# Layer norms of a two-layer decoder trunk: staged dummy products, squares on two engines, x from two queues, and no GpSimd work beside the norms

## The chip, the core and the metric

The kernel runs on one core of one Trainium2 chip. A core has five engines with a queue of instructions each: PE (matrix products; PEld is its weight load), DVE (vector), ACT (scalar and activation functions), POOL (GpSimd), and SP, which here only issues DMAs. The metric is the time of one execution in microseconds (us); before the change it is 2330.64 us, the median of 3 runs (2330.39 to 2331.34).

## The reference

Two layers (DEPTH = 2) over x of 256 tokens by 2048 channels, in float32. Each layer does

```
h = RMSNorm(x, pre_norm)                 # over the 2048 channels of a token
proj = h @ w_in                          # 2048 x 17120: three mixers and the merge gates
y_a = SSD(proj), y_b = RWKV-7(proj), y_c = sparse attention(proj)
merged = sum_i sigmoid(g_i + b_i) * (y_i @ w_branch_i)
x = x + RMSNorm(merged @ w_out, post_norm)
```

The change touches only the places where a token's sum of squares is taken and used: the norm ahead of the first layer, and the pair of norms between the two layers.

## The kernel before, in words

The 256 tokens are two halves of 128 (c = 0 and 1); a half of x is a tile of 128 partitions by 2048, named ya (c = 0) and yb (c = 1), which is worked on in four quarters of 512 columns (q = 0 to 3). A norm is: the squares of each quarter summed into a column of n_s (`square`, L808), a chain of eight one-column DVE instructions that makes 1/sqrt (`rstd`, L812, tiles n_x), the scaling of each quarter by it, and the transposition by PE (products with the identity in cst, 128 x 128, into PSUM tiles psa). From psa ACT makes hh (the rounded value) and DVE makes hl (the remainder), 16 pieces each of 128 x 256 (`prenorm`, L833).

All large products are done in three parts of a rounded format: hh with the rounded weight whi, hl with whi, and hh with the remainder wlo, accumulated in PSUM tiles psg. The weights come as 512 KB pieces (wraw) through SP's queue, in the order of use; each is two halves, of which `prepare` (L692) makes whi and wlo, each with four buffers. In the code before, the first three halves of the program have whi made by DVE and the others by ACT; wlo is made by POOL for the first six halves of a layer (PL = 6) and by DVE for the others.

PE's clock is one of two levels, 1.2 and 2.4 GHz; the profile's column PEclk gives it as 0.50 and 1.00. `warm` (L1615) issues products whose result is not used: six of 512 columns at the start, eight of 256 columns between the layers.

What order the instructions stand in is decided by a planner (`Program.issue`, L329): every call is recorded with its rank and the tiles that it reads and writes, and each engine then takes, at its own modelled time, the ready instruction of lowest rank (ranks: -2 and -1 before 0 before 1, 2, 3; equal ranks by the order in the code). `prenorm` has rank -1. The order is fixed when the program is built, and each engine works through its own list in that order. At the end of a layer `output` (L1552) makes the last columns of the product with w_out for the first half of the tokens, then for the second, and `add` (L1597) adds the normed result to x, half by half, writes it out and sums the next norm's squares.

Of the kernel before, what the change touches and what calls it, by code (L numbers as in the profile page):

```python
# [10 lines left out]
F32 = mybir.dt.float32  # L11
# [4 lines left out]
AF = mybir.ActivationFunctionType  # L16
OP = mybir.AluOpType
AX = mybir.AxisListType

DM, S, NL = 2048, 256, 2  # L20
# [9 lines left out]
LA = 2  # L30
# [2 lines left out]
PG = 3  # L33
KT = 2
KW = 2
PL = 6
KK = 14


# [65 lines left out]
CST = {"ident": 0, "tri": 128, "cbias": 256, "inv": 384, "sign": 385}  # L105
NCST = 386
# [98 lines left out]
class Program:  # L205
# [123 lines left out]
    def issue(self, tc):  # L329
# [21 lines left out]
        for i in range(N):  # L351
            if not left[i]:
                add(i)
# [18 lines left out]
        while len(order) < N:  # L372
# [74 lines left out]
            for j in users[i]:  # L447
                left[j] -= 1
                to = ops[j][0]
                ready[j] = max(ready[j], t + busy if to == e == "PE" else end[i] + (LT if to == "PE" else 0.0))  # L450
                if j in batch and batch.get(i) is not batch[j]:
                    batch[j][1] -= 1
                    batch[j][2] = max(batch[j][2], ready[j])
                if not left[j]:
                    add(j)
# [25 lines left out]
class Trunk:  # L481
# [82 lines left out]
        return y  # L564


    def setup(self):
        nc, v = self.nc, self.v
        self.ones = self.T([128, 128], "ones")
        v.memset(self.ones, 1.0)  # L570
        self.cst = self.T([128, NCST], "cst")
        self.io.dma_start(self.cst, self.cst_d[:, 0:NCST])
        c = lambda n, w=128: self.cst[:, CST[n]:CST[n] + w]
        self.ident, self.tri, self.cbias = c("ident"), c("tri"), c("cbias")
        self.blkr, self.onesr = [self.T([128, 128], n, dt=F32R) for n in ("blkr", "onesr")]
        blk = self.t1(128)
        self.io.dma_start(blk, self.cst_d[:, NCST:NCST + 128])
        v.tensor_copy(self.blkr, blk)
        v.tensor_copy(self.onesr, self.ones)

        self.zl = self.T([128, 10, S], "zl", dt=F32R)
        self.g.memset(self.zl.bitcast(F32), 0.0)

        self.zp = self.T([128, 6, 512], "zp")
        self.g.memset(self.zp, 0.0)

        self.sbd = self.T([128, 2, 128], "sbd")
        v.memset(self.sbd, 0.0)

        self.vd = self.T([128, 8, 128], "vd")  # L590
        self.g.memset(self.vd, 0.0)
        self.ut = self.T([128, 8, 64], "ut")
        v.memset(self.ut, 0.0)
# [98 lines left out]
    def prepare(self):  # L692

        self.prog.rank, was = 1, self.prog.rank
        while len(self.ready) <= LA and (self.raw or self.nraw < NL * self.wst.shape[1]):
            self.prog.rank = 1
            while len(self.raw) < 3 and self.nraw < NL * self.wst.shape[1]:
                self.fetch()
            r = self.raw.pop(0)
            of = 2 * self.wst.shape[1]  # L700
            n, self.nhalf = self.nhalf, self.nhalf + 1
            self.prog.rank = 1 if n > LA else -1
            if n % of < of - KK:
                hi = self.T([128, 512], "whi", WB, F32R)
                lo = self.T([128, 512], "wlo", WB, F32R)
                if n > LA:
                    self.s.activation(hi, r, AF.Copy)
                else:
                    self.v.tensor_copy(hi, r)
                (self.v if n % of >= PL else self.g).tensor_tensor(lo, r, hi.bitcast(F32), op=OP.subtract)  # L710
                self.ready.append((hi, lo))
                continue

            n = n % of - (of - KK)
            cut = lambda a: [a[:, 0:256], a[:, 256:512]]
            if n < KT:
                hi, lo = cut(self.t2(512, dt=F32R)), cut(self.t2(512, dt=F32R))
            elif n >= KK - KW:
                hi, lo = cut(self.T([128, 512], "whi", WB, F32R)), cut(self.T([128, 512], "wlo", WB, F32R))
            else:  # L720
                hi, lo = [[self.t1(dt=F32R) for _ in range(2)] for _ in range(2)]
            for e, q, h, w in zip((self.v, self.g), cut(r), hi, lo):
                self.s.activation(h, q, AF.Copy)
                e.tensor_tensor(w, q, h.bitcast(F32), op=OP.subtract)
            self.ready.append(list(zip(hi, lo)))
        self.prog.rank = was
# [70 lines left out]
            self.v.scalar_tensor_tensor(lo, src, scale, hi.bitcast(F32), op0=OP.mult, op1=OP.subtract)  # L797


    def residual(self, src):  # L800

        x = [self.T([128, DM], n) for n in ("ya", "yb")]
        for c in range(2):
            for q in range(4):
                self.io.dma_start(x[c][:, 512 * q:512 * q + 512], src[128 * c:128 * c + 128, 512 * q:512 * q + 512])
        return x

    def square(self, ss, x):  # L808

        self.s.activation(self.t2(512)[:, :x.shape[1]], x, AF.Square, scale=DM ** -0.5, accum_out=ss)  # L810

    def rstd(self, ss):  # L812
        v = self.v
# [783 lines left out]
    def add(self, x, u, ss, last, c):  # L1597
        v, s = self.v, self.s
        r = self.rstd(ss[c])
        so = self.sums(4)  # L1600
        cuts = [512 * i for i in range(5)]
        if last and c:
            cuts.insert(4, 1792)
        for q, qs in enumerate(slice(i, j) for i, j in zip(cuts, cuts[1:])):
            if c and q == 1:
                s.activation(u[c][:, qs], u[c][:, qs], AF.Copy, scale=r)
                self.g.tensor_tensor(x[c][:, qs], x[c][:, qs], u[c][:, qs], op=OP.add)
            else:
                v.scalar_tensor_tensor(x[c][:, qs], u[c][:, qs], r, x[c][:, qs], op0=OP.mult, op1=OP.add)
            self.io.dma_start(self.out[128 * c:128 * c + 128, qs], x[c][:, qs])  # L1610
            if not last:
                self.square(so[:, q:q + 1], x[c][:, qs])
        return so
# [6 lines left out]

    def run(self):
        self.prog.rank = 0
        x = u = self.residual(self.x_d)
        ss = [self.sums(4) for _ in range(2)]
        for c in range(2):
            for q in range(4):
                self.square(ss[c][:, q:q + 1], x[c][:, 512 * q:512 * q + 512])
        self.setup()
        self.warm(6, self.ones[:, None, :].to_broadcast([128, 4, 128]))
        self.prepare()  # L1630
        for l in range(NL):
            self.layer_setup(l)
            if l:
                self.prog.rank = 3
                self.warm(8, x[0][:, 1536:1792])
                self.prog.rank = 2
            h = self.prenorm(x, ss, u)
            if l == 0:
                self.rope_tables()
            m = self.layer(l, h)  # L1640
            x, ss, u = self.output(l, m)
        self.prog.issue(self.tc)
# [16 lines left out]
```

## Time and profile before

| what | value |
|---|---|
| median of the timed runs | 2330.64 us |
| the profiled execution, its own time | 2333.83 us |
| span of the profiled execution | 2332.1 us |
| PE busy in the span | 2295.8 us (98%), 18750 products |
| DVE, ACT, POOL busy | 1712.8, 1405.9 and 797.6 us (73%, 60%, 34%) |
| mean PE clock granted | 0.993 |

The profile is of one execution. A row of a timeline gives start, duration, engine, line, operation and tiles (out<-in), and in brackets how long the engine stood idle before it and what ended that. All rows have line 460, the planner's own, so rows are told apart by tiles.

### The profile page before, as it was taken

Reading aid. Unit: us, or ns where it says so; the run is one execution under the profiler, and the core shown is the slowest. Engines: PE = TensorE matmul, PEld = TensorE weight load, DVE = VectorE, ACT = ScalarE, POOL = GpSimd, SP = SyncE. Lnnn points to the kernel's source line nnn. Section 1 sums busy time; section 2 is a strip of 40 time slices with the busy share of each in tenths; the row PEclk is TensorE's granted clock in tenths of the full one; section 3 lists DMA queues with packets and bytes.
Section 4 is the critical chain, followed back from the end, with each engine's and each line's share of the span. In section 5 each row is a group of like instructions: output and inputs, shape, how many; then the busy total and the mean of one; then the engine's idle time right before and its main releaser. Section 6 shows DMA issues by size and latency. Waiting matters only on the chain. (4 is left out here: it accounts for less than half of the span.)

```text
span 2332.1 us, 50202 instructions
## 1 busy us (share of the span) xinstructions
PE 2295.8 (98%) x18750; PEld 2239.0 (96%) x18750; DVE 1712.8 (73%) x3468; ACT 1405.9 (60%) x2994; POOL 797.6 (34%) x1241
## 2 busy tenths in 40 slices
PE   8999999999999999999989999999999999999998
PEld 7999999999999999998889999999999999999987
DVE  7988998878995555556577789888789755555565
ACT  5876666775654454545467675776756544544453
POOL 3468564755210010101235776538341100110011
PEclk8999999999999999999999999999999999999999
DMA  5545453454445665556544545444454556655563
GB/s 187 177 159 184 126 175 118 138 159 152 142 163 187 221 207 185 200 185 214 170 145 157 177 152 161 125 138 156 141 162 140 172 188 219 206 189 191 183 216 127
DMA packets 149588, 396.14 MB, mean 170 GB/s; under 512 B 47904, under 2 KB 51936, under 8 KB 149088
## 3 DMA queue, kind: packets, MB, share of 16 engines
q1 hardware_dynamic: 149344, 392.94, 51.8%
q8 instruction: 147, 2.41, 0.4%
q14 instruction: 97, 0.79, 0.1%
HBM read 386.55 MB, written 6.32 MB: 168 GB/s over the span
## 5 line engine op out<-in xcount | busy, mean ns | idle before, releaser
L460 DVE TENSOR_TENSOR wlo<-wraw,whi 128x512 fp32r<-128x512 f32 x1352 | 1018.6, 756 | 528.3 <-ACT whi L460 515.6
L460 ACT ACTIVATE whi<-wraw 128x512 fp32r<-128x512 f32 x1361 | 857.4, 631 | 754.1 <-PE psg L460 707.9
L460 PE MATMUL psg<-hh,whi 128*128 128x256 f32 (+1 forms) x4224 | 1190.5, 282 | 1.0 <-ACT hh L460 1.0
L460 PE MATMUL psg<-hh,wlo 128*128 128x256 f32 (+1 forms) x4224 | 1190.1, 282 | 0.0
L460 PE MATMUL psg<-hl,whi 128*128 128x256 f32 (+1 forms) x4224 | 1186.6, 281 | 0.0
L460 PEld LDWEIGHTS psg<-hh,whi 128*128 128x128 f32 x4224 | 798.0, 189 | 2.4 <-ACT hh L460 1.6
L460 PEld LDWEIGHTS psg<-hl,whi 128*128 128x128 f32 x4224 | 798.3, 189 | 1.5 <-issue 0.8
L460 PEld LDWEIGHTS psg<-hh,wlo 128*128 128x128 f32 x4224 | 797.0, 189 | 1.8 <-issue 0.4
L460 POOL TENSOR_TENSOR t<-t,t 128x256 fp32r<-128x256 f32 (+22 forms) x506 | 340.5, 676 | 283.0 <-ACT t L460 170.4
L460 POOL TENSOR_TENSOR b_nm<-b_nm,t 128x256 f32<-128x256 f32 x64 | 51.2, 800 | 722.9 <-DVE t L460 714.9
L460 PE MATMUL psg<-t,whi 128*128 128x256 f32 x1536 | 280.6, 283 | 0.0
L460 PEld LDWEIGHTS psg<-t,whi 128*128 128x128 f32 x1536 | 238.9, 191 | 0.0
L460 PE MATMUL psg<-t,wlo 128*128 128x256 f32 x768 | 217.3, 283 | 0.0
L460 ACT ACTIVATE t<-t 64x256 fp32r<-64x256 f32 (+5 forms) x436 | 178.9, 416 | 35.1 <-DVE t L460 20.5
L460 PEld LDWEIGHTS psg<-t,wlo 128*128 128x128 f32 x768 | 147.1, 192 | 0.0
L460 POOL TENSOR_TENSOR t<-t,d 128x60 f32<-128x60 f32 (+24 forms) x248 | 108.1, 436 | 65.0 <-DMA d<-diag 27.6
L460 ACT ACTIVATE t<-psa 128x256 f32<-128x256 f32 (+5 forms) x230 | 93.8, 424 | 43.1 <-PE psa L460 41.8
L460 PE MATMUL psg<-whi,hh 128*128 128x512 f32 (+1 forms) x268 | 98.1, 366 | 0.0
L460 PE MATMUL psg<-wlo,hh 128*128 128x512 f32 (+1 forms) x268 | 97.7, 365 | 0.0
L460 PE MATMUL psg<-whi,hl 128*128 128x512 f32 (+1 forms) x268 | 97.1, 365 | 0.0
L460 PE MATMUL psa<-t,t 128*128 128x256 f32 (+1 forms) x384 | 87.5, 288 | 2.8 <-ACT t L460 2.2
L460 PE MATMUL psa<-t,zp 128*128 128x128 f32 (+1 forms) x448 | 82.3, 298 | 0.0
(248 smaller groups left out, 2503.4 us busy)
## 6 DMA issues: line engine op xcount, KB each, us to landing
wraw<-in_wst SPq DMA_DIRECT2D x688, 512.0 KB, 3.4
d<-diag SPq DMA_DIRECT2D x32, 128.0 KB, 3.8
t<-diag SPq DMA_DIRECT2D x16, 256.0 KB, 3.9
d<-in_wst SPq DMA_DIRECT2D x8, 512.0 KB, 4.9
ya<-in_x SPq DMA_DIRECT2D x8, 256.0 KB, 5.1
yb<-in_x SPq DMA_DIRECT2D x8, 256.0 KB, 6.1
b_nm<-in_post SPq DMA_DIRECT2D x2, 1024.0 KB, 4.8
out_x<-ya SPq DMA_DIRECT2D x8, 256.0 KB, 2.8
```

What stands on the lines that cost most here:

```text
L460: ops[i][2](*ops[i][3], **ops[i][4])
```

## The change

At the start, x is requested by two queues: quarters 1 and 3 of the second half of the tokens by ACT's queue, all others by SP's, and the constants (cst) are requested between the two halves of x. The squares of quarters 1 and 3 of each half go to DVE (as a product with a summed output), those of 0 and 2 stay on ACT. After the six dummy products come three further groups (2, 3 and 3, of 256 columns), each fed by the output of one of DVE's squares, so that it can't start before that. Between the layers the eight dummies are followed by groups of 5, 4 and 4, fed by quarters 0, 2 and 3 of the second half's new x.

All wlo are made by DVE and all whi by ACT (PL is gone), except in a layer's last pieces, and the first three halves have rank 0 where they had -1. In `add`, quarter 1 of the second half goes through ACT and POOL in the last layer alone; between the layers DVE does it. One constant (blkr) has rank 2.

```diff
@@ setup
+        self.prog.rank = 2
         blk = self.t1(128)
         self.io.dma_start(blk, self.cst_d[:, NCST:NCST + 128])
         v.tensor_copy(self.blkr, blk)
         v.tensor_copy(self.onesr, self.ones)
+        self.prog.rank = 0
@@ prepare
-            self.prog.rank = 1 if n > LA else -1
+            self.prog.rank = 1 if n > LA else 0
...
-                if n > LA:
-                    self.s.activation(hi, r, AF.Copy)
-                else:
-                    self.v.tensor_copy(hi, r)
-                (self.v if n % of >= PL else self.g).tensor_tensor(lo, r, hi.bitcast(F32), op=OP.subtract)
+                self.s.activation(hi, r, AF.Copy)
+                self.v.tensor_tensor(lo, r, hi.bitcast(F32), op=OP.subtract)
@@ residual
+            if c and between:
+                between()
             for q in range(4):
-                self.io.dma_start(x[c][:, 512 * q:512 * q + 512], src[128 * c:128 * c + 128, 512 * q:512 * q + 512])
+                (queues or [self.io])[c * q % 2 if queues else 0].dma_start(x[c][:, 512 * q:512 * q + 512], src[128 * c:128 * c + 128, 512 * q:512 * q + 512])
@@ add
-            if c and q == 1:
+            if c and last and q == 1:
@@ run
-        x = u = self.residual(self.x_d)
+        x = u = self.residual(self.x_d, [self.io, self.s], self.tables)
...
+                z = x[c][:, 512 * q:512 * q + 512]
+                if q % 2:
+                    sq.append(self.t2(512))
+                    self.v.tensor_tensor_reduce(out=sq[-1], in0=z, in1=z, scale=1.0 / DM, scalar=0.0, op0=OP.mult,
+                                                op1=OP.add, accum_out=ss[c][:, q:q + 1])
+                else:
+                    sq.append(self.square(ss[c][:, q:q + 1], z))
         self.setup()
         self.warm(6, self.ones[:, None, :].to_broadcast([128, 4, 128]))
+        for t, n in ((sq[3], 3), (sq[5], 2), (sq[7], 3)):
+            self.warm(n, t[:, 0:256])
...
-                self.warm(8, x[0][:, 1536:1792])
+                for n, a in ((8, x[0][:, 1536:1792]), (5, x[1][:, 0:256]), (4, x[1][:, 1024:1280]), (4, x[1][:, 1792:2048])):
+                    self.warm(n, a)
```

Since the planner decides on all of it at once, the order shifts elsewhere too: in the first layer many instructions stand in other places, in the second layer the lists come back to nearly the same order.

On DVE at the start of the program, before the change, the scaling of yb and the rounding of weights (whi) stand among each other, and the first remainders hl follow at once; wlo isn't in this list, it is POOL's.

```order
28 L460 TENSOR_SCALAR ya_63<-ya_63,n_x_111 128x512
29 L460 CAST whi_88<-wraw_86 128x512
30 L460 CAST whi_90<-wraw_86 128x512
31 L460 TENSOR_SCALAR yb_64<-yb_64,n_x_115 128x512
32 L460 CAST whi_93<-wraw_87 128x512
33 L460 TENSOR_SCALAR yb_64<-yb_64,n_x_115 128x512
34 L460 SCALAR_TENSOR_TENSOR hl_107<-psa_116,par_95,hh_106 128x256
35 L460 SCALAR_TENSOR_TENSOR hl_107<-psa_117,par_95,hh_106 128x256
36 L460 TENSOR_SCALAR d_oka_100<-par_95 128x8
```

In the changed list the same engine has its first wlo (wlo_92) only behind the last of the 16 hl; the first hl is row 41 there.

```order
56 L459 SCALAR_TENSOR_TENSOR hl_110<-psa_125,par_98,hh_109 128x256
57 L459 SCALAR_TENSOR_TENSOR hl_110<-psa_126,par_98,hh_109 128x256
58 L459 CAST t_66_128<-t_65_127 128x256
59 L459 SCALAR_TENSOR_TENSOR hl_110<-psa_125,par_98,hh_109 128x256
60 L459 SCALAR_TENSOR_TENSOR hl_110<-psa_126,par_98,hh_109 128x256
61 L459 TENSOR_TENSOR wlo_92<-wraw_89,whi_91 128x512
62 L459 TENSOR_TENSOR wlo_94<-wraw_89,whi_93 128x512
63 L459 TENSOR_TENSOR wlo_97<-wraw_90,whi_96 128x512
```

On PE at the same place, before, products of the first block (psg_134) stand among the transposes (psa), and the first with wlo is row 24.

```order
19 L460 MATMUL psg_134<-hh_106,whi_88 128x256
20 L460 MATMUL psa_120<-cst_76,yb_64 128x128
21 L460 MATMUL psa_120<-cst_76,ya_63 128x128
22 L460 MATMUL psa_120<-cst_76,yb_64 128x128
23 L460 MATMUL psg_134<-hl_107,whi_88 128x256
24 L460 MATMUL psg_134<-hh_106,wlo_89 128x256
25 L460 MATMUL psg_134<-hh_106,whi_88 128x256
26 L460 MATMUL psa_121<-cst_76,ya_63 128x128
```

In the changed list two products of the first block (rows 25 and 26) come ahead of the last twelve transposes, and the third needs wlo_92, with all others behind it.

```order
35 L459 MATMUL psa_126<-cst_65,ya_63 128x128
36 L459 MATMUL psa_126<-cst_65,yb_64 128x128
37 L459 MATMUL psa_126<-cst_65,ya_63 128x128
38 L459 MATMUL psa_126<-cst_65,yb_64 128x128
39 L459 MATMUL psg_137<-hh_109,wlo_92 128x256
40 L459 MATMUL psg_137<-hh_109,whi_91 128x256
41 L459 MATMUL psg_137<-hl_110,whi_91 128x256
42 L459 MATMUL psg_137<-hh_109,wlo_92 128x256
```

Between the layers, PE's changed list has eleven of the thirteen new dummies (into psa_3142, psa_3143 and psa_3144) ahead of the first transpose of the second half (row 8797); b_nm there is the scaled second half, yc the first.

```order
8789 L459 MATMUL psa_3141<-ya_2907,ones_76 128x256 x8
8790 L459 MATMUL psa_3142<-yb_2908,ones_76 128x256 x5
8791 L459 MATMUL psa_3143<-yb_2908,ones_76 128x256
8792 L459 MATMUL psa_3157<-cst_65,yc_2910 128x128
8793 L459 MATMUL psa_3143<-yb_2908,ones_76 128x256 x3
8794 L459 MATMUL psa_3144<-yb_2908,ones_76 128x256
8795 L459 MATMUL psa_3158<-cst_65,yc_2910 128x128
8796 L459 MATMUL psa_3144<-yb_2908,ones_76 128x256
8797 L459 MATMUL psa_3155<-cst_65,b_nm_2911 128x128
```

Before, nothing but two transposes of yc stood between the eight dummies of ya and that first transpose; the thirteen dummies of the second half are new.

## Rows read from the trace of the kernel before

**Rows 1.** Stretches, start: length; PE, PEld, DVE, ACT, POOL busy (instructions); clock, DMA, GB/s.

```profile
9.00:13.00 4.00, 0.75 (x6) 0.53 (x5) 3.41 (x20) 2.46 (x8) 0.00 (x0) 1.00 1.04 394
13.00:22.10 9.10, 6.53 (x24) 4.95 (x25) 7.91 (x14) 7.55 (x19) 8.04 (x10) 0.50 0.69 240
22.10:26.60 4.50, 4.50 (x23) 4.50 (x22) 3.59 (x13) 2.90 (x8) 1.19 (x3) 0.50 0.01 2
```

**Rows 2.** PE's psg products by stretch: busy (count), clock, DMA share, GB/s.

```profile
0.00:22.00 22.00, 2.13 (x5) 0.79 0.78 263
22.00:26.60 4.60, 3.59 (x14) 0.50 0.01 3
26.60:30.00 3.40, 3.40 (x31) 1.00 0.02 5
30.00:40.00 10.00, 10.00 (x88) 1.00 0.59 209
```

**Rows 3.** Timeline of DVE at the start.

```profile
9.57 1.28 DVE L460 TENSOR_SCALAR ya<-ya,n_x 128x512 f32<-128x512 f32 x3
...
11.34 0.16 DVE L460 TENSOR_REDUCE n_x<-n_s 128x1 f32<-128x5 f32 x1 [0.49 <-ACT t L460]
...
13.77 1.50 DVE L460 TENSOR_SCALAR yb<-yb,n_x 128x512 f32<-128x512 f32 x1
...
20.44 1.66 DVE L460 SCALAR_TENSOR_TENSOR hl<-psa,par,hh 128x256 fp32r<-128x256 f32 x4 [1.19 <-ACT hh L460]
```

**Rows 4.** Timeline of ACT at the start.

```profile
10.52 0.63 ACT L460 ACTIVATE t<-yb 128x512 f32<-128x512 f32 x1
...
12.89 1.34 ACT L460 ACTIVATE yb<-yb,n_x 128x512 f32<-128x512 f32 x2 [1.06 <-DVE n_x L460]
```

**Rows 5.** Timeline of POOL at the start.

```profile
13.60 5.62 POOL L460 TENSOR_TENSOR wlo<-wraw,whi 128x512 fp32r<-128x512 f32 x4 [6.73 <-DVE whi L460]
```

**Rows 6.** DMA issues of the first 12 us: size, us to landing.

```profile
cst<-in_cst SPq DMA_DIRECT2D x1, 193.0 KB, 6.4
```

**Rows 7.** A stretch between the layers, columns as in the first group.

```profile
1173.60:1176.90 3.30, 3.28 (x16) 3.28 (x17) 1.88 (x5) 2.88 (x7) 0.00 (x0) 0.50 0.01 2
```

**Rows 8.** Timeline of DVE between the layers.

```profile
1155.89 2.74 DVE L460 SCALAR_TENSOR_TENSOR ya<-yc,n_x,ya 128x512 f32<-128x512 f32 x4
...
1164.18 0.16 DVE L460 TENSOR_REDUCE n_x<-n_s 128x1 f32<-128x6 f32 x1 [1.18 <-ACT t L460]
...
1167.06 1.41 DVE L460 SCALAR_TENSOR_TENSOR yb<-b_nm,n_x,yb 128x512 f32<-128x512 f32 x2
1168.39 0.42 DVE L460 TENSOR_TENSOR b_nm<-psa,b_nm 128x256 f32<-128x256 f32 x1
...
1171.60 0.16 DVE L460 TENSOR_REDUCE n_x<-n_s 128x1 f32<-128x5 f32 x1 [1.46 <-ACT t L460]
```

**Rows 9.** Timeline of POOL between the layers.

```profile
1163.87 2.50 POOL L460 TENSOR_TENSOR wlo<-wraw,whi 128x512 fp32r<-128x512 f32 x2 [15.02 <-ACT whi L460]
```

**Rows 10.** Timeline of ACT between the layers.

```profile
1173.13 1.34 ACT L460 ACTIVATE b_nm<-yb,n_x 128x512 f32<-128x512 f32 x2 [1.57 <-DVE n_x L460]
```

**Rows 11.** Timeline of PE: dummies and first transpose between the layers, two waits later.

```profile
1163.26 3.62 PE L460 MATMUL psa<-ya,ones 128*128 128x256 f32 x16
...
1173.62 0.48 PE L460 MATMUL psa<-cst,b_nm 128*128 128x128 f32 x1 [4.43 <-DVE b_nm L460]
...
1227.76 0.41 PE L460 MATMUL psa<-adt,cst 128*128 128x32 f32 x2 [1.74 <-DVE adt L460]
...
1719.95 0.48 PE L460 MATMUL psa<-cst,t 128*128 128x128 f32 x1 [3.62 <-DVE t L460]
```

**Rows 12.** Stretches, same columns: the first layer's body, and behind a wait.

```profile
28.00:1163.00 1135.00, 1129.78 (x9302) 1105.24 (x9301) 848.88 (x1720) 692.95 (x1469) 390.92 (x612) 1.00 0.53 172
1227.70:1231.50 3.80, 3.74 (x19) 3.70 (x20) 2.38 (x7) 1.12 (x3) 0.00 (x0) 0.55 0.68 253
```

**Rows 13.** DVE's own wlo by line: shortest/median/longest ns, first and last start, forms.

```profile
L460 DVE TENSOR_TENSOR wlo<-wraw,whi x1352: 626/692/1782, 29.5 to 2298.2; 128x512 fp32r<-128x512 f32 x194
```

More of the change, by code (lines that the diff above doesn't have):

```diff
@@ L35 @@
 KW = 2
-PL = 6
 KK = 14
@@ L564, in rsqrt, with tables @@
         return y
+    def tables(self):
+        self.cst = self.T([128, NCST], "cst")
+        self.io.dma_start(self.cst, self.cst_d[:, 0:NCST])
+        c = lambda n, w=128: self.cst[:, CST[n]:CST[n] + w]
+        self.ident, self.tri, self.cbias = c("ident"), c("tri"), c("cbias")
     def setup(self):
@@ L570, in setup @@
         v.memset(self.ones, 1.0)
[L571 to L574, printed above, removed]
         self.blkr, self.onesr = [self.T([128, 128], n, dt=F32R) for n in ("blkr", "onesr")]
+        self.prog.rank = 2
         blk = self.t1(128)
@@ L797, in split, with residual @@
             self.v.scalar_tensor_tensor(lo, src, scale, hi.bitcast(F32), op0=OP.mult, op1=OP.subtract)
-    def residual(self, src):
+    def residual(self, src, queues=None, between=None):
         x = [self.T([128, DM], n) for n in ("ya", "yb")]
         for c in range(2):
+            if c and between:
+                between()
             for q in range(4):
-                self.io.dma_start(x[c][:, 512 * q:512 * q + 512], src[128 * c:128 * c + 128, 512 * q:512 * q + 512])
+                (queues or [self.io])[c * q % 2 if queues else 0].dma_start(x[c][:, 512 * q:512 * q + 512], src[128 * c:128 * c + 128, 512 * q:512 * q + 512])
         return x
     def square(self, ss, x):
-        self.s.activation(self.t2(512)[:, :x.shape[1]], x, AF.Square, scale=DM ** -0.5, accum_out=ss)
+        t = self.t2(512)[:, :x.shape[1]]
+        self.s.activation(t, x, AF.Square, scale=DM ** -0.5, accum_out=ss)
+        return t
     def rstd(self, ss):
@@ L1622, in run @@
         self.prog.rank = 0
-        x = u = self.residual(self.x_d)
+        x = u = self.residual(self.x_d, [self.io, self.s], self.tables)
         ss = [self.sums(4) for _ in range(2)]
+        sq = []
         for c in range(2):
             for q in range(4):
-                self.square(ss[c][:, q:q + 1], x[c][:, 512 * q:512 * q + 512])
+                z = x[c][:, 512 * q:512 * q + 512]
[5 more added lines that the diff above has]
+                    sq.append(self.square(ss[c][:, q:q + 1], z))
         self.setup()
         self.warm(6, self.ones[:, None, :].to_broadcast([128, 4, 128]))
+        for t, n in ((sq[3], 3), (sq[5], 2), (sq[7], 3)):
+            self.warm(n, t[:, 0:256])
         self.prepare()
```

## The prediction

> **What bounds the kernel now.** The table of busy times comes first: PE is busy for 2295.8 of 2332.1 us, and nothing in the change alters a product whose result is used. So it can move only where PE waits or works at half clock. I read the stretches next: in the first layer's body (28 to 1163 us) PE's idle time is 1135.00 - 1129.78 = 5.2 us [rows 12], so there is little to win there, and something to lose. What is left is the start and the seam between the layers. At the start PE is almost idle from 9 to 13 us (0.75 us busy), then 13 to 26.6 us pass at clock 0.50, the last 4.5 of them with PE full [rows 1]. At the seam PE waits 4.43 us for the scaled b_nm [rows 11] and then works 3.3 us full at 0.50 [rows 7]. The timelines of DVE, ACT and POOL then say what the norms wait for.
>
> All sums are made on the profiled execution, 2333.83 us (span 2332.1 and 1.7 outside it); it lies 3.2 us over the median 2330.64, and I carry the differences over to the median.
>
> **The start.** The progress of the first products (psg) is the measure. Before, 5 + 14 + 31 are begun by 30.0 us; up to three stand in two stretches, so about 47. From there the rate is 88 in 10 us, 0.117 us each [rows 2].
>
> What the norm waits for before: ACT's last square starts at 10.52 [rows 4] and the sum of the second half at 11.34 [rows 3]; the scaling starts at 12.89 on ACT [rows 4], so the chain takes 1.5 us.
>
> The x transfers: cst (193.0 KB) [rows 6] now goes ahead of the second half. At 394 GB/s [rows 1] that is 0.198 MB / 394 = 0.5 us later for the last quarter, and I keep it whole although two queues issue, because the share of the DMA engines already is 1.04 in that stretch [rows 1]. The sum then comes at about 11.9, the scale at 13.45.
>
> Beside this row stands a rule of the Trainium skill ("DMA: Bandwidth & Descriptors", section "Issuing engines are not separate DMA queues"): transfers issued by several engines go through the same 16 DMA engines and interleave, so several issuers save issue time only. The 1.04 agrees with it, and by the rule the last quarter doesn't land sooner. Were it otherwise and the two queues added their rates, x would land some 0.8 us sooner and the forecast would be 2328.7.
>
> DVE's four squares: no row shows this operation. The nearest are DVE's wlo at 0.69 (same size) [rows 13] and DVE's scaling beside POOL's work at 1.50 [rows 3]. Four cost 2.8 to 6.0 us; I take 0.75 each, by the row without company, since POOL now has nothing there. At that price three are done while x is still landing, and the last lies beside ACT's square of 0.63 [rows 4]: cost 0. At 1.50 the last ends 0.8 later than ACT's and the one ahead of it may push it: up to 1.3 us. Below nothing it can't cost beyond the 0.6 of one ACT square.
>
> Behind the sum: on DVE the three ya scalings at 0.427 (1.28 for three) [rows 3], two of yb at the same price (0.86; it was 1.50 for one beside POOL [rows 3, 5]), two small ones (0.2): 13.45 + 2.3 = first hl at 15.75. Sixteen hl at 1.66 / 4 = 0.415 [rows 3] are 6.6, four small instructions 0.5: 22.9. Only now comes wlo_92 (it was POOL's, at 1.4 us each, 5.62 for four [rows 5]; DVE's takes 0.69 [rows 13]): 23.6. In PE's new order the third product waits for it, so PE's list is free at about 23.75. Then all weights and remainders are there. At full clock the 47th product begins 44 x 0.117 = 5.15 later, at 28.9: 1.1 us sooner than before.
>
> But the clock: PE now has dummies to about 12.6 (eight of the kind that took 3.62 us between the layers [rows 11], 9.0 + 3.6), and from there to 23.75 only some 34 short instructions, about 4 us of work in 11. Before, with PE busy 6.53 of 9.10 us between 13.0 and 22.1, the clock was 0.50 all along, and it was regained only behind 4.5 us of full work [rows 1]. So I expect half clock by 23.75, and to be regained by full work as long as in the three places seen: 4.5 [rows 1], 3.3 [rows 7], 3.8 us at 0.55 [rows 12]. In each, half the time is lost: 1.65 to 2.25, I take 2.0. The start costs **-1.1 + 2.0 = +0.9**. Its ends: -1.1 with the clock up, -1.8 with earlier x too; +2.5 with slow squares.
>
> **The seam.** POOL's two wlo run from 1163.87 for 2.50 us [rows 9]. Beside them the first half's norm needs 1164.18 to 1167.02, where yb's scaling follows at 1167.06 [rows 8]: 2.84 instead of the 1.5 of the start. Without POOL: one wlo more on DVE (1163.9 to 1164.6), the chain to 1166.05, three adds at 2.74 / 4 = 0.685 [rows 8] to 1168.1, the product's evacuation at 0.42 [rows 8] to 1168.5, the fourth add (before on ACT and POOL) to 1169.15, ACT's square and the sum at about 1170.05: 1.55 sooner than 1171.60 [rows 8]. By the same 2.02 from sum to first b_nm transpose (1171.60 to 1173.62 [rows 8, 11]) this is ready at 1172.05.
>
> PE's eight dummies end at 1163.26 + 3.62 = 1166.9 [rows 11]; eleven new ones at 0.45, held up by the adds that feed them, go to about 1171.9. So they hardly delay the transpose, PE isn't idle for long, and the half clock at 1173.6 to 1176.9 [rows 7] goes: 1.65. Next in line is ACT, whose two b_nm scalings take 1.34 [rows 10]; behind them it makes hh from about 1173.0. The fifth product of the next block, at 1178.7 before (my reading of PE's products there), comes at 1176.7: **-2.0**. Its ends: -2.8 if the whole of 1.55 and 1.65 is kept, -0.5 if the dummies overrun or the clock falls all the same.
>
> **Elsewhere.** Six wlo per layer go from POOL to DVE, 4.2 us each layer of an engine that is busy 848.88 of 1135 [rows 12]: hidden as long as nobody waits for it. The wait for adt (1.74) and for t (3.62) in the second layer [rows 11] have the same neighbours in the lists afterwards: they stay. Layer 0's new order I price at 0, with its loss as a rival.
>
> **Sum.** +0.9 - 2.0 + 0 = -1.1: 2332.7 on the profiled execution, **2329.5 us** on the median.
>
> **Rivals.**
> *A, slower: layer 0's new order brings a wait.* DVE has the wlo and also the small chains (dt, adt) for which PE waits at [rows 11]; layer 0, with 5.2 us idle [rows 12], has no such wait now, and its list is the one that is reshuffled. One like adt's costs 1.74 and half of the 3.8 us at half clock behind it [rows 12], 3.5; one like t's 3.62 + 1.7 = 5.3. Time 2333.0 to 2334.8, with two 2336.5. It decides from about 1 us of net loss in layer 0. Against it: PE's order is planned against the same costs as before, and 75% of DVE's time is used, not all.
> *B, the dummies at the start hold the clock*: -1.1 instead of +0.9, 2327.5, with x sooner or both ends of the seam 2326. For it: the clock was 1.00 in 9 to 13 with PE nearly idle [rows 1], so it doesn't fall at once. Against it: 13 to 22.1 at 0.50 with PE 72% busy.
> *C, the seam gives little*: the thirteen dummies, fed one after the other by the adds, push the transposes, or the clock falls in the hh stage behind them. -0.5 instead of -2.0: 2331.0.
> That layer 0's new order wins is bounded by the 5.2 us idle in it; I give it no case, but room in the range.
>
> **How the numbers follow.** Forecast 0.47, A 0.18, B 0.20, C 0.15. What a measurement here can tell from no change is about 0.2%, 4.7 us: below 2326.0 and above 2335.3. Faster: half of B and some of the forecast's lower tail (layer 0 a little better), 0.18. Slower: most of A, 0.14. Within: 0.68. The forecast's own range is 2327.3 to 2332; with B below and A above, and the unknown price of the squares, 2325.3 to 2335.5.
>
> **What would show it.** Start: the sum of the second half at 11.9 (sooner: the queues do add up), DVE's squares near 0.75, first hl at 15.8, wlo_92 at 22.9, PE's third product at 23.75, clock 0.50 before and for some 4 us behind it, then 1.00. If the clock is 1.00 there, B. Seam: no POOL, the sum at 1170, the first b_nm transpose at 1172 behind the dummies, no stretch at 0.50. Elsewhere: the waits of 1.74 and 3.62 still there, and layer 0's idle time near 5 us. The forecast is wrong if layer 0 shows a wait of over 1.5 us, if DVE's squares take twice as long, or if the first block's third product stands at another time than 23 to 24.5 us.

## The result, and the profile after

The changed kernel takes 2350.6 us (median of 4 runs, 2347.32 to 2351.51) beside 2330.99 us of the kernel before (4 runs): ratio 1.008, 95% interval 1.0064 to 1.0096. It is slower by 19.6 us; the forecast was 2329.5, the range ended at 2335.5.

To see where the time went I cut each profiled execution at three instructions that every kernel has: the 48th psg product at the start, the first dummy of the seam, and the 48th psg product behind it. The body is the first layer between the first two. Idle is its length less PE's busy time; half is the time at clock 0.50 in it, by the trace's clock record.

| us | 48th product at | body | idle in it | half in it | seam | from there to the end |
|---|---|---|---|---|---|---|
| before | 30.03 | 1133.23 | 5.22 | 0 | 20.49 | 1148.33 |
| after | 30.18 | 1151.16 | 15.55 | 17.1 | 18.26 | 1145.95 |
| difference | +0.2 | **+17.9** | +10.3 | +17.1 | -2.2 | -2.4 |

The differences add up to 13.5, which is that of the two spans (2345.6 and 2332.1). The medians lie 19.6 apart: the profiled run of the changed kernel is its shortest, at 2347.32, and that of the kernel before is longer than its median, so some 6 us of the difference stand in neither trace. In the body PE's busy time is 7.6 us longer for the same work; 14.2 us of work at half clock (4.3, 3.4 and 6.4 us in the three stretches at 0.50) accounts for about 7 of them. The two places that the change edits come out as forecast, at the start even to a few tenths. First DVE there, with start, duration and what it did:

```profile
8.59 0.69 DVE L459 CUSTOM_DVE_ANT_0 t<-ya 128x512 f32<-128x512 f32 x1
...
12.15 0.15 DVE L459 TENSOR_REDUCE n_x<-n_s 128x1 f32<-128x5 f32 x1
...
15.77 1.66 DVE L459 SCALAR_TENSOR_TENSOR hl<-psa,par,hh 128x256 fp32r<-128x256 f32 x4
...
22.80 3.02 DVE L459 TENSOR_TENSOR wlo<-wraw,whi 128x512 fp32r<-128x512 f32 x4
```

The square costs 0.69 (I took 0.75), the sum of the second half comes at 12.15 (11.9), the first hl at 15.77 (15.75), wlo_92 at 22.80 (22.9). Where [rows 3] had the sum at 11.34, it is 0.8 later. PE has its dummies to 12.35, then little, and waits for that wlo:

```profile
8.73 3.62 PE L459 MATMUL psa<-t,ones 128*128 128x256 f32 x16
...
23.53 0.58 PE L459 MATMUL psg<-hh,wlo 128*128 128x256 f32 x1 [3.81 <-DVE wlo L459]
```

The clock is at 0.50 from 22.97 to 26.39, so PE works at it for 2.86 us behind the wait. At the seam there is no POOL and no half clock (stretches; columns as in [rows 1]), and what [rows 11] showed as a wait of 4.43 us for b_nm is now dummies up to the first transpose:

```profile
1184.80:1190.00 5.20, 5.20 (x26) 4.23 (x25) 4.77 (x15) 3.29 (x9) 0.00 (x0) 1.00 0.81 251
1190.00:1195.20 5.20, 5.20 (x43) 4.88 (x43) 4.35 (x11) 5.04 (x14) 0.00 (x0) 1.00 0.15 53
```

```profile
1187.58 1.89 PE L459 MATMUL psa<-yb,ones 128*128 128x256 f32 x8
...
1189.97 0.33 PE L459 MATMUL psa<-cst,b_nm 128*128 128x128 f32 x1
```

The loss is in the body, where the change edits nothing but who makes six wlo. What PE waits for there, between 30 and 1160 us (total, times, longest), before:

```profile
PE psa L460 <- ACT zp L460: 1.1, 2, 0.6
PE psa L460 <- POOL zl L460: 0.9, 1, 0.9
```

and after:

```profile
PE psa L459 <- DMA vd<-diag: 6.5, 1, 6.5
PE psa L459 <- POOL t L459: 2.4, 1, 2.4
PE psa L459 <- DVE t L459: 2.4, 5, 1.2
PE psa L459 <- ACT t L459: 1.8, 5, 0.4
PE psg L459 <- DVE yb L459: 1.7, 1, 1.7
```

They lie close together, between 351 and 419 us:

```profile
351.19 0.39 PE L459 MATMUL psg<-hh,whi 128*128 128x256 f32 x1 [1.66 <-DVE yb L459]
...
363.41 1.94 PE L459 MATMUL psa<-cst,vd 128*128 128x128 f32 x8 [6.47 <-DMA vd<-diag]
...
380.30 0.71 PE L459 MATMUL psa<-b_nm,zp 128*128 128x128 f32 x4 [1.16 <-DVE t L459]
```

vd is the end of a long chain of the RWKV mixer (`rwkv_inverse`): a matrix is written to DRAM (diag<-b_nm) and read back (d), POOL solves a triangular system in 62 short instructions, the result goes through DRAM again (diag<-t, vd<-diag), and PE transposes it. The chain runs twice in the layer; this is the second round. Before, d is requested at 278.20 and POOL begins at 284.51; after, at 301.41 and 309.10. First the rows of before:

```profile
278.20 1.71 SPq L460 DMA_DIRECT2D d<-diag  x4
...
334.76 0.34 SPq L460 DMA_DIRECT2D vd<-diag  x1
```

```profile
284.51 0.23 POOL L460 TENSOR_TENSOR t<-t,d 128x31 f32<-128x31 f32 x1
...
322.49 0.80 POOL L460 TENSOR_TENSOR t<-t,t 128x8 f32<-128x8 f32 x1
```

```profile
342.93 1.03 PE L460 MATMUL psa<-cst,vd 128*128 128x128 f32 x8
```

And after:

```profile
301.41 0.80 SPq L459 DMA_DIRECT2D d<-diag  x2
...
354.52 2.52 SPq L459 DMA_DIRECT2D diag<-t  x4
358.46 0.34 SPq L459 DMA_DIRECT2D vd<-diag  x1
```

```profile
309.10 0.92 POOL L459 TENSOR_TENSOR t<-t,d 128x31 f32<-128x31 f32 x1 [12.38 <-DMA d<-diag]
...
354.28 0.22 POOL L459 TENSOR_TENSOR t<-t,t 128x8 f32<-128x8 f32 x1
```

The chain stands 23 us later in the new order, and POOL, with other work among the solve's instructions, needs 45.4 us for it (309.10 to 354.50), 38.8 before (284.51 to 323.3). Before, the same transposes ran at 342.93 without a wait, but the last piece of vd had landed only at 342.12: the chain had 0.8 us of room. After, it lands at 363.21, and the transposes start at 363.41. Behind the waits PE works at half clock (the first row is the wait itself):

```profile
356.90:363.40 6.50, 0.04 (x1) 0.02 (x1) 0.04 (x1) 0.63 (x1) 0.00 (x0) 0.81 0.33 51
360.90:367.70 6.80, 4.29 (x20) 4.32 (x21) 0.69 (x1) 1.19 (x2) 0.00 (x0) 0.50 0.47 115
```

### The profile page after: what moved, and what is told of

Same layout as the page of the kernel before. It is cut to its first block, busy times and chain, and to the rows that moved or that the text cites. A ratio compares the mean times of both kernels' runs of the same rounds, so it can differ in the third digit from the quotient of the medians.

```text
span 2345.6 us, 50270 instructions
## 1 busy us (share of the span) xinstructions
PE 2304.6 (98%) x18792; PEld 2246.1 (96%) x18792; DVE 1719.5 (73%) x3486; ACT 1398.8 (60%) x2986; POOL 784.0 (33%) x1228
## 5 line engine op out<-in xcount | busy, mean ns | idle before, releaser
L459 POOL TENSOR_TENSOR t<-t,t 64x256 fp32r<-64x256 f32 (+24 forms) x506 | 341.6, 679 | 284.4 <-ACT t L459 166.8
L459 POOL TENSOR_TENSOR zl<-t,t 64x256 fp32r<-64x256 f32 x76 | 64.2, 845 | 61.6 <-ACT t L459 49.2
```

The source lines that it names most:

```text
L459: ops[i][2](*ops[i][3], **ops[i][4])
```

## The experiments

Theory 1: the 17.9 us are the first layer's new order, an accident of the planner. Theory 2: they are the edits, with DVE doing POOL's wlo. In all of them the ratio is to runs of the kernel before in the same job (medians 2331.98 to 2333.2). The rows' line is the planner's own in each kernel, from 459 to 472.

**Old order, new edits; new order, old edits.** A list of the planned order is stored in the kernel and replaces the planner's. The body's part of it is taken from the other kernel's plan; start, seam and second layer keep their own.

```diff
+STORED = "..."
...
+        order = stored()
         with tc.manual_schedule():
             for i in order:
```

> All edits of the change, but in the first layer's body (behind the start, ahead of the seam between the layers) every engine's list stands in the order of the kernel before. Theory 1 (the loss is the body's new order: POOL's solve chain ends late, its way through DRAM follows, and PE waits for vd): the 17.9 us lost in the body go, the start keeps +0.2 and the seam -2.2, so 2327 to 2330 us beside about 2331 of the kernel before, and no wait of PE over 1.5 us between 30 and 1160 us. Theory 2 (the edits themselves, above all the wlo that DVE makes in POOL's place, load the engines of the first layer): still slower than 2343.

Measured: 2330.96 us, ratio 0.9994 (0.9986 to 1.0003); body 1131.70, idle 3.92, longest wait in it 0.94 us. The 17.9 us are gone from the body.

> The kernel before without any edit, but its first layer's body in the order of the changed kernel. Theory 1: the loss comes without the edits: 2331 + 18 = about 2349 us (2345 to 2353), with a wait of 5 to 7 us for vd near 360 us. Theory 2: the order is worth nothing, 2330 to 2333.

Measured: 2353.98 us, ratio 1.0092 (1.0078 to 1.0106); body 1154.28, idle 15.11. Without one edit, the order brings the loss and the wait (both just outside what I gave: the time 1 us above, the wait 0.1 below):

```profile
363.49 1.94 PE L472 MATMUL psa<-cst,vd 128*128 128x128 f32 x8 [4.88 <-DMA vd<-diag]
```

So the order alone bears the loss, and theory 2 falls. The first run lies 1 us above the range I gave, beside a kernel before that stands at 2332.47 in this job: the seam keeps its gain (18.28), but the part behind it takes 1148.28 us, not 1145.95, though its lists are those of the changed kernel, instruction for instruction. Nor did the start keep its +0.2: the 48th product stands at 31.64. There ACT's first whi, which stands ahead of its scalings of yb and waits for the weights to land, begins at 13.86 (13.38 in the changed kernel), PE's transposes run at clock 0.50 from 15.72 to 19.14 (1.00 there), and the third product follows at 24.71 (23.53).

**The seam alone.**

```diff
-            if c and q == 1:
+            if c and last and q == 1:
...
-                self.warm(8, x[0][:, 1536:1792])
+                for n, a in ((8, x[0][:, 1536:1792]), (5, x[1][:, 0:256]), (4, x[1][:, 1024:1280]), (4, x[1][:, 1792:2048])):
+                    self.warm(n, a)
```

> The kernel before with the seam's two edits alone (thirteen more dummies, quarter 1 of the second half's add on DVE); wlo stays on POOL there and no list of the first layer changes. Both theories: the seam gains 1.5 to 2.2 us, and up to 2.4 more where the waits in the second layer are followed by full clock: 2326.5 to 2329.5. If the gain of the seam came from POOL's missing wlo rather than from these two edits, 2330.5 to 2331.5.

Measured: 2332.66 us, ratio 1.0001 (0.9993 to 1.001); seam 19.43 (20.49 before), without half clock. By this, half of the seam's 2.2 us comes from these two edits. For the other half POOL's missing wlo is the likely cause: here POOL makes its two from 1162.07 to 1164.57, and the first half's chain on DVE takes 2.88 us from its sum to yb's scaling (1162.38 to 1165.26), beside 1.46 in the changed kernel (1182.51 to 1183.97), where POOL stands still. One instruction of that chain, here and in the changed kernel:

```profile
1163.39 1.19 DVE L460 SCALAR_TENSOR_TENSOR n_x<-n_x 128x1 f32<-128x1 f32 x1
```

```profile
1183.13 0.16 DVE L459 SCALAR_TENSOR_TENSOR n_x<-n_x 128x1 f32<-128x1 f32 x1
```

No run takes POOL's wlo away alone. The expected gain in the whole time isn't there: 1.1 us are less than this comparison resolves.

**The start alone.** The change's part in setup, residual and run, up to the dummies; whi, wlo and seam as before.

```diff
-        x = u = self.residual(self.x_d)
+        x = u = self.residual(self.x_d, [self.io, self.s], self.tables)
...
+        for t, n in ((sq[3], 3), (sq[5], 2), (sq[7], 3)):
+            self.warm(n, t[:, 0:256])
```

> The kernel before with the start's edits alone (two queues, cst between the halves, squares on DVE, staged dummies, blkr's rank); wlo and whi as before. The first layer's lists come out in a third order. Theory 1: the start itself is worth within 1 us of nothing, but the third order may lose as much as the second: anything from 2331 to 2355, and the loss is found as waits of PE between 100 and 700 us. Theory 2: no wlo moved to DVE, so 2330 to 2332.

Measured: 2358.35 us, ratio 1.011 (1.0096 to 1.0124); body 1156.02, idle 20.84, of it one wait of 9.11 us for vd at 370.96. A third order, 3.4 us dearer than the worst I had allowed, without any wlo moved. The 48th product is at 31.93, 1.9 later than before, since PE waits 6.48 us ahead of its transposes, so the start isn't within 1 us of nothing in this form.

**One number of the planner.** The modelled delay behind an instruction of DVE, ACT or SP is changed by one nanosecond, in the last of three runs by three (137); every instruction is the same.

```diff
-LD = 140
+LD = 139
```

> The changed kernel with one number of the planner's model altered (LD, the delay it assumes behind an instruction of DVE, ACT or SP, 139 instead of 140 ns); all instructions are the same, only the order differs. It was chosen because the planner itself takes this plan to end earlier. Theory 1 (the loss is an accident of the order, not of the edits): the first layer's body, from the 48th product to the dummies of the seam, falls from 1151.2 to 1131 to 1137 us, and the whole to 2327 to 2335. Theory 2 (an order that suits the edits doesn't exist, since DVE has more to do): 2343 or more.

Measured, on the changed kernel: 2326.97 us, ratio 0.998 (0.9971 to 0.9989). Body 1133.03, idle 4.08; the longest wait in it is 0.65 us. It lies 23.6 us below the changed kernel (of another job) and 5.0 below the kernel before of its job. The body only comes back to what it was before (1133.23); what the trace shows as gained is in the seam (18.27) and in the second layer (1141.78 from there to the end), where the wait of 3.62 us for t [rows 11] has gone. PE's waits in the body now begin with

```profile
PE psa L459 <- ACT t L459: 2.2, 5, 0.7
```

> The kernel before with the same one number altered (139 for 140) and no other edit. Theory 1: its order was a lucky one, so another costs 3 to 15 us: 2334 to 2346, with waits of PE between 230 and 500 us that the kernel before doesn't have. Rival: the planner's order is robust without the change, and the change alone upset it: 2330 to 2333.

Measured, on the kernel before: 2344.9 us, ratio 1.0057 (1.0044 to 1.0071); body 1147.91, idle 15.22. The same wait comes back, in the chain's first round, as 3.81 of the 10 us by which the idle time grew:

```profile
237.32 0.39 PE L460 MATMUL psg<-hh,whi 128*128 128x256 f32 x1 [1.40 <-DVE yb L460]
245.34 1.94 PE L460 MATMUL psa<-cst,vd 128*128 128x128 f32 x8 [3.81 <-DMA vd<-diag]
```

One nanosecond in a model moves either kernel by 13 to 24 us, in opposite directions.

> The kernel before with the number at 137: no edit of the change, a plan that the planner takes to end early. Theory 1 (once both have a good order, the change is worth the seam's 2.2 us and little more): body 1131 to 1134, seam 20.5, and 2328 to 2332. If the change itself bore the gain of 5 us in the run with 139, this one stays at 2331 to 2333; if orders alone did, it comes to 2326 to 2328.

Measured, on the kernel before with 137: 2327.68 us, ratio 0.9981 (0.9972 to 0.999); body 1133.19, seam 21.63, and 1143.84 from there (1148.33 before): its gain is in the second layer, where the wait of 3.62 us for t has gone here too. The time lies 0.3 below theory 1's range, in the range for orders alone. So an order is worth as much to the kernel before as to the changed one; with one good order for each, the change itself shows no difference (0.998 and 0.9981).

**The solve made shorter**, in the changed kernel's own order:

```diff
         for r in range(31):
...
+            if not short or r < 16:
```

> The changed kernel in its own order; the second of the first layer's triangular solves on POOL leaves out rows 16 to 30 (30 instructions, about 13 us of POOL's work), which leaves out part of the computation. Theory 1 (the wait of 6.5 us for vd is the solve's end plus its way through DRAM): the diag writes move up to where SP's list lets them, behind the wraw that is issued at 350.8 instead of 354.5, and the wait becomes about 3 us; with the shorter half clock 4 to 6 us in all: 2345 to 2347 beside 2350.6. Rival (PE waits for the DMAs themselves, whose issue takes 0.5 us each and whose way takes 2 us): wait and time stay.

Measured: 2347.6 us, ratio 1.0069 (1.0053 to 1.0084); body 1148.01.

```profile
351.72 2.53 SPq L471 DMA_DIRECT2D diag<-t  x4
355.68 0.34 SPq L471 DMA_DIRECT2D vd<-diag  x1
```

```profile
360.73 1.73 PE L471 MATMUL psa<-cst,vd 128*128 128x128 f32 x8 [3.28 <-DMA vd<-diag]
```

As theory 1 had it, the wait falls by 3.2 us (body: 3.15), to the point where SP's list, no longer POOL, lets the writes go; the half clock behind it got shorter (3.4 us, 6.8 before), but of the 6.8 PE had worked only 4.3, so little was saved by it, and the time is 0.6 above the range. Half of the wait is the solve's end; that the other half is SP's place in the order and the way through DRAM follows from the rows, but no run takes it away.

**The first wlo on POOL**, with the stored old order in the body:

```diff
-                self.v.tensor_tensor(lo, r, hi.bitcast(F32), op=OP.subtract)
+                (self.v if n > LA else self.g).tensor_tensor(lo, r, hi.bitcast(F32), op=OP.subtract)
```

> As the run with all edits and the old order in the first layer's body, but the first three halves' wlo are made by POOL again. Theory S (at the start PE's third product waits for wlo_92 alone, 3.8 us, because DVE has it behind sixteen hl): the 48th product, at 31.6 us in that run and 30.2 in the changed kernel, comes at 26 to 28, and the whole takes 2326 to 2328.5. Rival: POOL slows DVE as in the rows of before (1.50 us for a scaling of 0.43), the hl end later by as much: 48th product at 30 or later, 2330 or more.

Measured: 2329.34 us, ratio 0.9992 (0.9983 to 1.0), 48th product at 28.33, so the start gains 3.3 us against the 31.64 of the first run (1.9 against the 30.18 of the changed kernel). The product misses theory S's range by 0.3 us and the rival's by 1.7, so at the start theory S holds; the time lies between the two ranges, 0.8 above the one and 0.7 below the other, and decides nothing. The start's gain is partly given back (body 1133.51, 1131.70 in that run), at a product for which the first run didn't wait:

```profile
41.10 0.64 PE L471 MATMUL psa<-t,ones 64*64 64x256 f32 x2 [1.78 <-ACT t L471]
```

**Both together**: that edit, in the order that 139 gave, stored.

```diff
+STORED = "..."
...
+                (self.v if n > LA else self.g).tensor_tensor(lo, r, hi.bitcast(F32), op=OP.subtract)
```

> The changed kernel in the order that the altered number gave, with the first three halves' wlo on POOL at the start. If the two gains add up, 48th product at 28.3 us (30.3 without POOL's wlo), body about 1133 us, and 1.5 to 2 us less than 2327.0 (beside a kernel before of 2332.0): 2324.5 to 2326.5 beside 2332. If the start's gain is given back further on (the weights come no sooner), 2326 to 2328.

Measured: 2326.11 us, ratio 0.997 (0.9959 to 0.9981), the lowest of all, though its interval overlaps that of the run with 139 (0.9971 to 0.9989). But 48th product at 26.42 (30.28 without POOL) and body 1137.34 (1133.03): all 3.9 us won at the start are lost again in the body, 2.53 of them at once:

```profile
40.04 0.64 PE L471 MATMUL psa<-t,ones 64*64 64x256 f32 x2 [2.53 <-ACT t L471]
```

with half clock from 41.59 to 45.00 behind it. By its time this run lies in both ranges, which overlap; by its stretches it shows the second case: what the start won was given back 14 us later, at a product that needs a result of ACT and DVE, not of POOL.

## Why the prediction was wrong

- The step that failed is "Layer 0's new order I price at 0, with its loss as a rival". It costs 17.9 us in the trace: 10.3 idle and about 7 by half clock. Both swaps of the order and the one-nanosecond runs show it.
- Rival A had the right layer and sign and the wrong place and size. I looked for a wait behind DVE's small chains (dt, adt), 3.5 to 5.3 us, because those were the waits that the trace of before showed [rows 11]. The new order is late in a chain that had no wait before: POOL's solve and two ways through DRAM. A chain without a wait isn't one with room: before, vd landed 0.8 us ahead of its use, and the new order puts the chain some 23 us later but its use only 14 (356.94 without the wait).
- The bound that I took from "5.2 us idle" [rows 12] speaks only of what can be won. Nothing in the trace of before bounds what another order can lose; my argument against A, that the planner works with the same costs, was no bound either: the kernel before with 139 loses 13 us by the same planner and costs.
- The start came out about as forecast: +0.9, and +0.2 between the two profiled executions, where every instant of its chain came within 0.3 us. The regained clock cost less than the 2.0 I took (half of 2.86 us is 1.4), and the third product came 0.2 earlier. One execution of each doesn't settle it closer: with the start's lists of before the 48th product also stood at 29.39 and 29.42 (the new order without edits, and the seam alone), with those of the changed kernel at 30.22 (the shorter solve), and with one instruction of DVE more at 31.64, so the start costs from 0.2 to 2.2 us.
- The rule on issuing engines (the Trainium skill, "DMA: Bandwidth & Descriptors", section "Issuing engines are not separate DMA queues") is in agreement with the trace: with two queues the last quarter of x lands at 11.14, 10.49 before, and ACT's last square starts at 11.16, 10.52 before [rows 4]. So x didn't land sooner; it landed later by about what cst ahead of it was taken to cost.
- The seam was right: -2.0 forecast, -2.2 measured, sum at 1187.95 and first transpose 2.02 behind it, as taken. With the same lists the seam also took 21.24 and 20.55 before (the new order without edits, and the start alone) and 18.27 to 18.28 after, so its gain is 2.2 to 3.0.
- "Elsewhere" was wrong in a second place: the waits of 1.74 and 3.62 us in the second layer stayed as forecast (1.30 and 3.62), but in this execution no half clock followed them. By the other runs the -2.4 is luck of this execution and no gain of the change: three other kernels with the same list of the second layer take 1148.28 to 1149.50 us there, and the list of before takes 1148.11 to 1148.33 in three.

## What to carry to other kernels

Where one program orders all instructions, an edit at the start is two changes: the edit, and a new draw of the order; price the second by what other orders cost, not at zero, or fix the order and compare. An edit should be judged against a kernel before that has had the same number of tries at an order. Ahead of a forecast, list the long chains that end just in time (here one over POOL and DRAM), with the room that each has, not only those for which something waits.

## What was not expected of the hardware

The clock behind one and the same wait differs between executions of one and the same list. Four kernels run the second layer in the same order, instruction for instruction: the changed kernel, the new edits in the old order, the shorter solve and the first wlo on POOL. In each PE waits 3.62 us for t. Behind that wait the clock was 0.50 not at all in the first, for 6.8 us in the second, and for 3.4 in the other two; those two had another 3.4 behind the wait for adt. From the seam to the end the four took 1145.95, 1148.28, 1148.66 and 1149.50 us: up to 3.6 us between executions. What decides it no run here shows. Runs of one kernel lie 2 to 6 us apart (2330.09 to 2336.22 in 21 runs of the kernel before); the clock may well be one reason, but no kernel was profiled twice.

What remains open: why an order puts the chain 23 us later. The planner's steps from the first differing instruction to that place weren't followed.
